# A routed trunk layer: second norm on VectorE and ScalarE, early expert splits on VectorE, and a re-ordered routing stage

## The chip, the cores and the metric

The kernel runs on one core of one Trainium2 chip. The metric is the device time of one execution in microseconds; the median of the runs counts. A trace names five engines: PE (TensorE matmuls; PEld is its weight load), DVE (VectorE), ACT (ScalarE), POOL (GpSimd) and SP (SyncE, which here only issues DMAs). Each engine works through a queue of its own, in order.

## What is computed

One layer on 1024 tokens of width 1024 in float32: a token mixer, a cross-attention into 256 memory tokens, and a mixture of 16 experts of which each token takes two. Each is followed by a residual norm. The part that matters here, cut from the reference:

```python
x = layer_norm(ALPHA * x + xa, ln_x_g, ln_x_b)         # second norm
scores = sigmoid(x @ router_w)                          # [T, 16]
sel = scores + router_bias
grp_score = top_k(sel.reshape(T, 4, 4), 2)[0].sum(-1)   # best of 4 groups
in_grp = group_of_expert == argmax(grp_score)
_, idx = top_k(where(in_grp, sel, -inf), 2)             # two experts in it
gate = take(scores, idx); gate = gate / gate.sum(-1)
y = sum over the two experts of gate * (silu(x@wg) * (x@wu)) @ wd
x = layer_norm(ALPHA * x + y, ln_moe_g, ln_moe_b)
```

Tokens are sorted by expert into blocks of 128 rows; a block is one gather, two matmul groups and one scatter with addition.

## The kernel before, in words

Tokens go in 8 tiles of 128. Every float32 product is three matmuls of a high and a low part (lines 78 to 80), so every operand is split: ACT copies the high part (line 74), another engine subtracts to get the low part (line 75).

The stage in question runs from the attention output to the first expert blocks. Its order is written out by hand: `at(time, fn, ...)` (line 600) files a step under a nominal time, and `run_agenda` (line 603) emits all steps sorted by it, so the nominal times fix the order within each engine's queue and nothing else. Steps of tile t:

- `p_turn`, `p_hi`, `p_lo` (from line 1212): transposed attention weights and their split. `xa` (line 1223): 48 matmuls into a PSUM tile; tile 7 is done in two halves (`xa_half`).
- Second norm. `n_sum` (line 1235) adds the residual on DVE, `n_stats` takes mean and variance on DVE (`bn_stats`), `n_scale` (line 1260) is one power on POOL. Then for tiles 0 to 5 `n_shift` (DVE), `n_norm` (ACT, line 1268), `n_affine` (POOL, line 1272) and `n_add` (POOL for tiles 0 to 3, DVE for 4 and 5; line 1275); for tiles 6 and 7 `n_vec`, two DVE passes (lines 1280 and 1281).
- `x_store`, `a_scale`, `a_store`: normed rows to DRAM, and scaled rows to the result buffer.
- Routing. `r_turn`, `r_copy`, `r_logits`, `r_score`: transpose, 16 small matmuls, sigmoid. `r_group` and `r_pick` (lines 874 and 889): 15 small DVE steps that choose two experts. `r_rank`: a small matmul with the counts so far. `r_place` (line 962, its steps from line 916): some 22 DVE steps that turn ranks into one-hot rows; `r_list` and `r_add` add them to the slot lists.
- After tile 3: `f_counts` to `f_gather` (from line 1034) choose three experts, fill two blocks from the first 512 tokens, and start weight loads (`f_load`, `fetch_some`: three register loads and five 1 MB DMAs on SP).
- `e_split` (line 1369) splits the 12 weight pieces of the first two experts: ACT for the high part, POOL for the low. `eb_*` are the two early blocks (products into `gup`, gate, transpose, fold, products into `yp`, scatter).
- After tile 7, placing is woven with `order_steps` (line 1160), then `o_sum`, `o_lists`, `o_index`, `o_gather` (from line 1176) give the slot lists and gather the next block. From there 20-odd blocks follow in a program order of the framework's own scheduler.

Of the kernel before, what the change touches and what calls it, by code (L numbers as in the profile page):

```python
# [9 lines left out]
F32 = mybir.dt.float32  # L10
F32R = mybir.dt.float32r
BF16 = mybir.dt.bfloat16
# [27 lines left out]
NEARLY = 3  # L40


@with_exitstack
def trunk_kernel(ctx: ExitStack, tc: tile.TileContext, a, out):
# [555 lines left out]
    def at(time, fn, *args):  # L600
        agenda.append((time, len(agenda), fn, args))
# [272 lines left out]
    def r_group(t):  # L874
        R = routes[t]
        sel, q, h = tt(f"rsel{t}", NE), tt(f"rq{t}", 12), tt(f"rh{t}", 8)
        R["sel"], R["g8"], R["gi"], R["gf"] = sel, tt(f"rg{t}", 8), tt(f"rgi{t}", 8, U32), tt(f"rgf{t}", 1)
        vec.tensor_tensor(sel, R["s"], rb, op=ALU.add)
        pr = sel[:, :].rearrange("p (g a b) -> p g a b", g=4, a=2)
        q3, h3 = q[:, :].rearrange("p (g a) -> p g a", a=3), h[:, :].rearrange("p (g a) -> p g a", a=2)  # L880
        vec.tensor_tensor(h3, pr[:, :, :, 0], pr[:, :, :, 1], op=ALU.max)
        vec.tensor_tensor(q3[:, :, :2], pr[:, :, :, 0], pr[:, :, :, 1], op=ALU.add)
        vec.tensor_tensor(q3[:, :, 2], h3[:, :, 0], h3[:, :, 1], op=ALU.add)
        vec.reduce_max(gs8[:, :4], q3, axis=AX.X)
        vec.max(R["g8"], gs8)
        vec.max_index(R["gi"], R["g8"], gs8)
        vec.tensor_copy(R["gf"], R["gi"][:, :1])

    def r_pick(t):
        R = routes[t]  # L890
        pen, ms_ = tt(f"rpen{t}", 4), tt(f"rms{t}", NE)
        vec.tensor_scalar(pen, iota16[:, :4], R["gf"], -BIG, op0=ALU.not_equal, op1=ALU.mult)
        vec.tensor_tensor(ms_[:, :].rearrange("p (g a) -> p g a", g=4), R["sel"][:, :].rearrange("p (g a) -> p g a", g=4),
                          pen[:, :, None].to_broadcast([P, 4, 4]), op=ALU.add)
        e8, ei, ef = tt(f"re{t}", 8), tt(f"rei{t}", 8, U32), tt(f"ref{t}", 2)
        vec.max(e8, ms_)
        vec.max_index(ei, e8, ms_)
        vec.tensor_copy(ef, ei[:, :2])
        oh, ohs = tt(f"roh{t}", NE), tt(f"rohs{t}", NE, BF16)
        vec.tensor_scalar(oh, iota16, ef[:, :1], None, op0=ALU.is_equal)  # L900
        vec.scalar_tensor_tensor(ohs, iota16, ef[:, 1:2], oh, op0=ALU.is_equal, op1=ALU.add)
        R["ef"], R["ohs"] = ef, ohs
# [13 lines left out]
    def place_steps(t):  # L916
# [27 lines left out]
        yield lambda: r_count(t)  # L944
# [86 lines left out]
    # the first experts are chosen, and two blocks filled, from the tokens seen by then  # L1031
# [40 lines left out]
    def f_close():  # L1072
# [3 lines left out]
        vec.tensor_copy(gce, m[:, NE + 2:NE + 4])  # L1076
        fill = first["fill"]
# [3 lines left out]
        first.update(idx=ixe, gate=gce)  # L1081
# [156 lines left out]
    def n_tiles(t):  # L1238
        S["ln", t] = [tiny.tile([P, n], F32, tag=g, name=f"{g}_n2_{t}") for g, n in (("mv", 2), ("sc", 1), ("nb", 1))]
        S["st", t] = tiny.tile([P, 2, 6], F32, tag="st", name=f"st_n2_{t}")  # L1240

    def n_moments(t):
        mv, sc, _ = S["ln", t]
        vec.bn_aggr(mv, S["st", t])
        vec.tensor_scalar(sc, mv[:, 1:2], EPS, None, op0=ALU.add)

    def n_stats(t):
        n_tiles(t)
        for k in range(2):
            vec.bn_stats(S["st", t][:, k, :], x2(t)[:, k * 512:k * 512 + 512])  # L1250
        n_moments(t)

    def n_half(k):
        if k == 0:
            n_tiles(7)
        cols = slice(k * 512, k * 512 + 512)
        vec.scalar_tensor_tensor(x2(7)[:, cols], x1(7)[:, cols], ALPHA, S["xa", 7][:, cols], op0=ALU.mult, op1=ALU.add)
        vec.bn_stats(S["st", 7][:, k, :], x2(7)[:, cols])

# [4 lines left out]
    def n_shift(t):  # L1264
        mv, sc, nb = S["ln", t]
        vec.scalar_tensor_tensor(nb, mv[:, :1], -1.0, sc, op0=ALU.mult, op1=ALU.mult)

    def n_norm(t):
        mv, sc, nb = S["ln", t]
        act.activation(x2(t), x2(t), AF.Identity, bias=nb, scale=sc)  # L1270

    def n_affine(t):
        pool.tensor_tensor(x2(t), x2(t), gb2[0], op=ALU.mult)

    def n_add(t):
        (pool if t < 4 else vec).tensor_tensor(x2(t), x2(t), gb2[1], op=ALU.add)

    def n_vec(t):
        mv, sc, nb = S["ln", t]
        vec.scalar_tensor_tensor(x2(t), x2(t), mv[:, :1], gb2[0], op0=ALU.subtract, op1=ALU.mult)  # L1280
        vec.scalar_tensor_tensor(x2(t), x2(t), sc, gb2[1], op0=ALU.mult, op1=ALU.add)
# [11 lines left out]
    B0 = 15.0  # L1293
    for t in range(NT):
        B = B0 * t
        end = B + B0
        if t:
            at(B - 8.1, p_turn, t)
            at(B - 7.1, p_hi, t)
            at(B - 7.0, p_lo, t)  # L1300
        for j, o in enumerate((0, 3.0, 4.3, 5.6, 7.8, 9.5, 10.8, 13.0)):
# [5 lines left out]
        if t < 7:  # L1307
            at(end + 0.1, n_sum, t)
            at(end + 0.2, n_stats, t)
        else:  # L1310
            at(end - 0.5, n_half, 0)
            at(end + 0.1, n_half, 1)
            at(end + 0.2, n_moments, t)
        at(end + 0.3, n_scale, t)
        if t < 6:
            at(end + 3.25, n_shift, t)
            at(end + 3.3, n_norm, t)
            at(end + 4.0, n_affine, t)
            at(end + 7.5, n_add, t)
            x, lg, group, pick, _, rank, place, late = (end + o for o in (10.6, 16.3, 18.1, 18.3, 21.3, 24.1, 24.6, 29.3))  # L1320
        elif t == 6:
            at(end + 0.4, n_vec, t)
            x, lg, group, pick, _, rank, place, late = (end + o for o in (6.0, 16.5, 20.8, 20.9, 20.95, 22.0, 22.2, 25.5))
        else:
            at(end + 0.4, n_vec, t)
            x, lg, group, pick, _, rank, place, late = (end + o for o in (5.3, 7.8, 10.8, 11.0, 12.95, 12.9, 13.3, 16.0))
        at(x + 0.1, x_store, t)
        turn_at = x + 0.3 if t == 7 else end + (12.1 if t < 6 else 15.2)
        at(turn_at, r_turn, t)
        at(turn_at + 1.0, r_copy, t)  # L1330
        at(turn_at + 2.0, a_scale, t)
        at(turn_at + 3.0, a_store, t)
        at(lg, r_logits, t)
        at(lg + 1.7, r_score, t)
        at(group, r_group, t)
        at(pick, r_pick, t)
        at(rank, r_rank, t)
        if t < 7:
            at(place, r_place, t)
        else:  # L1340
            at(place, lambda: r_place(7, order_steps()))
        at(late, r_list, t)
        if t < 7:
            at(late + (3.6 if t < 6 else 6.1), r_add, t)
        if t == 3:
            f = late + 3.7
            at(rank + 1.0, f_counts)
            at(rank + 4.0, f_choose)
            at(f + 0.1, f_slots)
            at(f + 0.2, f_bonus)  # L1350
# [3 lines left out]
            at(f + 0.5, f_load)  # L1354
            at(f + 0.6, fetch_some, 5)
# [21 lines left out]
    at(E - 14.5, early_splits)  # L1377
# [3 lines left out]
    for n, k in enumerate((6, 7, 8, 9)):  # L1381
        at(E + (-7.0, 0.35, 0.4, 0.45)[n], e_split, k, pool)
    for n, k in enumerate((4, 5, 10, 11)):
        at(E + 2.0 + 3.6 * n, e_split, k, pool)
# [37 lines left out]
    for n, base in ((0, E - 13.0), (1, E - 6.0)):  # L1422
        at(base, eb_turn, n)
        at(base + (1.0 if n else 1.4), eb_parts, n)
    for j in range(NK):
        at(E + (0.15, 0.2, 1.45, 1.46, 1.47, 5.0, 5.75, 5.76)[j], eb_hidden, 0, j)
# [200 lines left out]
```

## Time and profile before

| | us |
|---|---|
| median of 3 runs (994.6 to 996.63) | 996.24 |
| profiled execution, span from first to last instruction | 991.4 |
| its PE busy | 910.8 (92%) |
| its DVE busy | 584.9 (59%) |
| its ACT busy | 410.9 (41%) |
| its POOL busy | 304.2 (31%) |

The profiled execution has no time of its own beside its span; the median lies 4.8 us above the span, which is what lies around the first and the last instruction. Matmuls are pipelined and overlap in the records, so a busy PE says that work was queued. A row of a timeline is start, duration, engine, line, operation, output<-inputs, shapes and count, and in brackets the idle time before it with what ended it.

### The profile page before, as it was taken

Reading aid. Unit: us, or ns where it says so; the run is one execution under the profiler, and the core shown is the slowest. Engines: PE = TensorE matmul, PEld = TensorE weight load, DVE = VectorE, ACT = ScalarE, POOL = GpSimd, SP = SyncE. Lnnn points to the kernel's source line nnn. Section 1 sums busy time; section 2 is a strip of 40 time slices with the busy share of each in tenths; the row PEclk is TensorE's granted clock in tenths of the full one; section 3 lists DMA queues with packets and bytes.
Section 4 is the critical chain, followed back from the end, with each engine's and each line's share of the span. In section 5 each row is a group of like instructions: output and inputs, shape, how many; then the busy total and the mean of one; then the engine's idle time right before and its main releaser. Section 6 shows DMA issues by size and latency. Waiting matters only on the chain. (4 is left out here: it accounts for less than half of the span.)

```text
span 991.4 us, 13027 instructions
## 1 busy us (share of the span) xinstructions
PE 910.8 (92%) x4841; PEld 774.9 (78%) x4841; DVE 584.9 (59%) x1154; ACT 410.9 (41%) x640; POOL 304.2 (31%) x221
## 2 busy tenths in 40 slices
PE   8999999999899999999999999987589999999910
PEld 8999778788677889998888888876468888888710
DVE  5300374546876785272224558979957677676528
ACT  5311432245422144352224432234237667767524
POOL 0211243226453314201111042325732323333226
PEclk9999999999999999999999999999799999999965
DMA  8200011113421357420001012173549898898364
GB/s 304 83 22 22 22 65 43 64 32 128 170 75 54 107 194 273 150 86 0 1 1 43 1 43 86 64 310 108 190 128 347 298 317 290 281 296 270 51 196 167
DMA packets 35439, 133.41 MB, mean 135 GB/s; under 512 B 6640, under 2 KB 8240, under 8 KB 29232
## 3 DMA queue, kind: packets, MB, share of 16 engines
q1 hardware_dynamic: 28464, 115.79, 32.3%
q0 software_dynamic: 6912, 16.79, 7.2%
q8 instruction: 38, 0.62, 0.2%
q14 instruction: 25, 0.20, 0.1%
HBM read 115.75 MB, written 25.20 MB: 142 GB/s over the span
## 5 line engine op out<-in xcount | busy, mean ns | idle before, releaser
L75 DVE TENSOR_TENSOR ew<-raw,ew 128x1024 fp32r<-128x1024 f32 x84 | 101.5, 1223 | 21.7 <-ACT ew L74 20.8
L74 ACT ACTIVATE ew<-raw 128x1024 fp32r<-128x1024 f32 x96 | 100.3, 1057 | 19.4 <-PE xa L80 9.7
L78 PE MATMUL gup<-ew,xbT 128*128 128x512 f32 x192 | 79.2, 412 | 0.0
L1146 POOL DMA_INDIRECT yd<-y,idx x22 | 41.5, 1884 | 122.2 <-ACT ew L74 46.2
L79 PE MATMUL gup<-ew,xbT 128*128 128x512 f32 x192 | 76.7, 399 | 0.0
L80 PE MATMUL gup<-ew,xbT 128*128 128x512 f32 x192 | 76.7, 399 | 0.0
L78 PE MATMUL zB<-xs,wb 128*128 128x512 f32 x192 | 76.5, 399 | 0.0
L80 PE MATMUL zB<-xs,wb 128*128 128x512 f32 x192 | 76.1, 396 | 0.0
L79 PE MATMUL zB<-xs,wb 128*128 128x512 f32 x192 | 75.0, 391 | 0.0
L78 PE MATMUL xa<-vws,T_p 128*128 128x512 f32 x128 | 53.9, 421 | 0.0
L78 PE MATMUL mixp<-wm,mx 128*128 128x512 f32 x128 | 53.2, 415 | 0.0
L79 PE MATMUL mixp<-wm,mx 128*128 128x512 f32 x128 | 50.9, 398 | 0.7 <-DVE wm L75 0.7
L79 PE MATMUL xa<-vws,T_p 128*128 128x512 f32 x128 | 51.4, 401 | 0.0
L80 PE MATMUL xa<-vws,T_p 128*128 128x512 f32 x128 | 51.3, 401 | 0.0
L80 PE MATMUL mixp<-wm,mx 128*128 128x512 f32 x128 | 50.9, 398 | 0.0
L78 PE MATMUL sc<-As,T_x 128*128 128x512 f32 x128 | 50.9, 398 | 0.0
L80 PE MATMUL sc<-As,T_x 128*128 128x512 f32 x128 | 50.4, 394 | 0.0
L79 PE MATMUL sc<-As,T_x 128*128 128x512 f32 x128 | 50.2, 392 | 0.0
L791 POOL TENSOR_TENSOR pss<-pss,nm 128x1024 f32<-128x1024 f32 x8 | 15.1, 1894 | 113.2 <-DVE nm L789 113.2
L80 PEld LDWEIGHTS gup<-ew,xbT 128*128 128x128 f32 x192 | 36.8, 192 | 8.5
L78 PEld LDWEIGHTS gup<-ew,xbT 128*128 128x128 f32 x192 | 37.0, 193 | 7.9 <-issue 0.6
L79 PEld LDWEIGHTS zB<-xs,wb 128*128 128x128 f32 x192 | 36.1, 188 | 8.9 <-issue 0.5
(447 smaller groups left out, 2505.2 us busy)
## 6 DMA issues: line engine op xcount, KB each, us to landing
raw<-in_wgu SPq DMA_DIRECT2D x32, 1024.0 KB, 8.2
raw<-in_wdn SPq DMA_DIRECT2D x16, 1024.0 KB, 7.4
raw_wk<-in_wkv SPq DMA_DIRECT2D x16, 512.0 KB, 4.5
wbr<-in_wB SPq DMA_DIRECT2D x12, 512.0 KB, 3.2
xt<-in_x SPq DMA_DIRECT2D x8, 512.0 KB, 3.2
raw_wq<-in_wxqT SPq DMA_DIRECT2D x8, 512.0 KB, 4.2
xd<-x2s SPq DMA_DIRECT2D x8, 512.0 KB, 3.3
yd<-xal SPq DMA_DIRECT2D x8, 512.0 KB, 2.8
```

Source lines behind the costliest of these rows:

```text
L74: act.activation(hi, src, AF.Copy)
L75: sub.tensor_tensor(lo, src, hi.bitcast(F32), op=ALU.subtract)
L78: pe.matmul(ps, lhi, rhi, start=first, stop=False)
L79: pe.matmul(ps, lhi, rlo, start=False, stop=False)
L80: pe.matmul(ps, llo, rhi, start=False, stop=last)
L791: pool.tensor_tensor(pr4, pr4, nm[:, 1, :, None].to_broadcast([P, H, M]), op=ALU.mult)
L1146: pool.indirect_dma_start(out=yd[:, :], out_offset=bass.IndirectOffsetOnAxis(ap=ix, axis=0), in_=y[:, :D], in_offset=None, bounds_check=T ...
```

## The change

It touches this stage only. In words:

- Second norm of tiles 0 to 6: `n_sum` also gives the row sum, ACT squares the centred rows (`n_square`, written over the attention output in PSUM), DVE does `n_var`, `n_centre` and `n_vec`. POOL keeps the power alone. Tile 7 keeps `bn_stats`.
- The low parts of the 12 early weight pieces are subtracted on DVE (`vec`), at new places in the order.
- `r_group` and `r_pick` become one list of steps. For tile 7 it is woven with the placing steps of tile 6. `place_part` also runs for tile 6.
- `r_count` leaves the placing and follows `r_rank`.
- Times: tiles 15.4 apart instead of 15.0; transposes of the attention weights some 3 earlier; logits of a tile one tile earlier; early-expert choice and weight loads before the place of tile 3; the early blocks' steps and the two products of the second one later. `eb_store(0)` comes before `o_gather`, `eb_out(1)` after it.

Core of the diff:

```diff
+MOVES = {('e_split', k): -1.50 for all 12 k, ('place_last',): 2.50, ('xa', 5, 3): -1.00}
...
 def at(time, fn, *args):
+    time += MOVES.get((fn.__name__, *[a for a in args if isinstance(a, int)]), 0.0)
...
+    def r_choose(t):
+        beside = list(place_steps(t - 1)) if t == 7 else []
+        for n, step in enumerate(choose_steps(t)):
+            step()
+            for _ in range(2 if n % 2 and beside else 1):
+                if beside:
+                    beside.pop(0)()
+        for step in beside:
+            step()
...
     def n_sum(t):
-        vec.scalar_tensor_tensor(x2(t), x1(t), ALPHA, S["xa", t], op0=ALU.mult, op1=ALU.add)
+        vec.scalar_tensor_tensor(x2(t), x1(t), ALPHA, S["xa", t], ..., accum_out=sc)
+        vec.tensor_scalar(mv[:, :1], sc, -1.0 / D, None, op0=ALU.mult)
+    def n_square(t):
+        act.activation(S["xa", t], x2(t), AF.Square, bias=mv[:, :1], accum_out=mv[:, 1:2])
+    def n_var(t):
+        vec.tensor_scalar(sc, mv[:, 1:2], 1.0 / D, EPS, op0=ALU.mult, op1=ALU.add)
-    def n_norm(t):
-        act.activation(x2(t), x2(t), AF.Identity, bias=nb, scale=sc)
-    def n_affine(t):
-        pool.tensor_tensor(x2(t), x2(t), gb2[0], op=ALU.mult)
-    def n_add(t):
-        (pool if t < 4 else vec).tensor_tensor(x2(t), x2(t), gb2[1], op=ALU.add)
+    def n_centre(t):
+        vec.scalar_tensor_tensor(x2(t), x2(t), mv[:, :1], gb2[0], ...)
     def n_vec(t):
-        vec.scalar_tensor_tensor(x2(t), x2(t), mv[:, :1], gb2[0], op0=ALU.subtract, op1=ALU.mult)
         vec.scalar_tensor_tensor(x2(t), x2(t), sc, gb2[1], op0=ALU.mult, op1=ALU.add)
...
-    B0 = 15.0
+    B0 = 15.4
         if t < 7:
+            at(end + 22.6, place_part, t, 0)
+            at(end + 22.65, place_part, t, 1)
...
-    for n, k in enumerate((0, 1, 2, 3)):
-        at(E - 13.5 + 1.4 * n, e_split, k, pool)
...
+    for k, o in zip((0, 1, 2, 3, 6, 7, 8, 9, 4, 5, 10, 11), (-20.5, -18.5, -7.5, -7.4, -2.0, 2.2, 9.0, 13.5, 17.2, 17.3, 23.1, 23.2)):
+        at(E + o, e_split, k, vec)
```

In the new order the DVE queue from the end of tile 6's attention product reads: choice of tile 5, list of tile 4, norm of tile 6, count, low part of block 0, splits 2 and 3, placing of tile 5, first half of tile 7's sum, split 6, low part of block 1, choice of tile 6, list of tile 5, second half of tile 7's sum, `n_centre`, split 7, `n_vec`, count, gate product of block 0, placing of tile 6, split 8, fold of block 0, choice of tile 7 with a second placing of tile 6, split 9, count, splits 4 and 5, placing of tile 7 with the order steps, list of tile 6, gate product of block 1, `o_sum`, splits 10 and 11, `o_index`.

## Rows read from the trace of the kernel before

**Rows 1.** The page, busy tenths in 40 slices of the span and the granted clock

```profile
DVE  5300374546876785272224558979957677676528
POOL 0211243226453314201111042325732323333226
PEclk9999999999999999999999999999799999999965
```

**Rows 2.** Stretches: us, then busy PE, PEld, DVE, ACT, POOL; PEclk, DMA share, GB/s

```profile
662.40:687.60 25.20, 18.73 (x85) 15.20 (x84) 24.22 (x62) 9.92 (x12) 14.29 (x6) 0.86 0.58 197
687.60:732.60 45.00, 30.95 (x143) 24.84 (x144) 37.35 (x124) 13.81 (x18) 22.39 (x11) 0.85 0.33 117
732.60:945.00 212.40, 210.96 (x1045) 173.15 (x1046) 142.84 (x159) 143.95 (x173) 65.80 (x43) 0.99 0.83 264
```

**Rows 3.** Waits of PE from 640 to 735: total us, times, longest

```profile
PE rp L906 <- DVE rohs L901: 12.7, 2, 8.1
```

**Rows 4.** Timeline of DVE and of POOL around the second norm of tile 6

```profile
667.25 1.28 DVE L1280 SCALAR_TENSOR_TENSOR x2s<-x2s,mv_n,g 128x1024 f32<-128x1024 f32 x1
669.00 3.40 DVE L1281 SCALAR_TENSOR_TENSOR x2s<-x2s,sc_n,b 128x1024 f32<-128x1024 f32 x1 [0.46 <-POOL sc_n L1262]
...
667.42 1.54 POOL L1262 TENSOR_TENSOR sc_n<-sc_n,mhalf 128x1 f32<-128x1 f32 x1 [8.86 <-DVE sc_n L1245]
668.95 5.70 POOL L75 TENSOR_TENSOR ew<-raw,ew 128x1024 fp32r<-128x1024 f32 x2
```

**Rows 5.** DVE groups by shape, 662.4 to 723.5: busy us, mean ns | idle before

```profile
L1281 DVE SCALAR_TENSOR_TENSOR x2s<-x2s,sc_n,b 128x1024 f32<-128x1024 f32 x2 | 6.8, 3390 | 0.9 <-POOL sc_n L1262 0.9
L940 DVE TENSOR_SCALAR one<-iota,rpm,rgp 128x128 fp32r<-128x128 f32 x13 | 5.8, 502 | 0.0
L878 DVE TENSOR_TENSOR rsel<-rs,rb 128x16 f32<-128x16 f32 x3 | 3.9, 1313 | 0.0
L892 DVE TENSOR_SCALAR rpen<-iota,rgf 128x4 f32<-128x4 f32 x3 | 3.3, 1091 | 0.1
L957 DVE TENSOR_TENSOR rgp<-rgt,rgp 128x2 fp32r<-128x2 f32 x4 | 2.9, 721 | 0.0
L900 DVE TENSOR_SCALAR roh<-iota,ref 128x16 f32<-128x16 f32 x3 | 2.7, 913 | 0.1
L883 DVE TENSOR_TENSOR rq<-rh 128x4 f32<-128x4 f32 x3 | 2.6, 865 | 0.0
L881 DVE TENSOR_TENSOR rh<-rsel 128x8 f32<-128x8 f32 x3 | 2.6, 863 | 0.1
L898 DVE CAST ref<-rei 128x2 f32<-128x2 uint32 x3 | 2.3, 763 | 0.1
...
L937 DVE TENSOR_SCALAR one<-iota,rcd 128x128 fp32r<-128x128 f32 x8 | 2.2, 281 | 0.0
...
L882 DVE TENSOR_TENSOR rq<-rsel 128x8 f32<-128x8 f32 x3 | 0.5, 159 | 0.0
```

**Rows 6.** Timeline of DVE: a split's subtraction, a placing, the next sum

```profile
659.73 1.22 DVE L1221 TENSOR_TENSOR T_p<-tp_p,T_p 128x1024 fp32r<-128x1024 f32 x1
660.86 0.23 DVE L929 SCALAR_TENSOR_TENSOR rjunk<-iota,ref,rs 128x16 f32<-128x16 f32 x1
...
664.37 1.21 DVE L1236 SCALAR_TENSOR_TENSOR x2s<-x1s,xa 128x1024 f32<-128x1024 f32 x1
```

**Rows 7.** Timeline of ACT: first sigmoid's table load; a squaring in the last stage

```profile
585.04 1.28 ACT L872 ACT_TABLE_LOAD   x1
959.94 1.15 ACT L1550 ACTIVATE zscratch<-yl,zs 128x1024 f32<-128x1024 f32 x1 [0.47 <-DVE zs L1548]
```

**Rows 8.** Timeline of PE: two router products, and the next block's transposes

```profile
647.14 1.85 PE L867 MATMUL rp<-rw,x2T 128*128 128x16 f32 x16
710.81 3.43 PE L867 MATMUL rp<-rw,x2T 128*128 128x16 f32 x16
...
732.63 2.71 PE L390 MATMUL tp_xb<-ident,xbs 128*128 128x128 f32 x11 [2.10 <-DMA xbs<-xd,idx]
```

More of the change, by code (lines that the diff above doesn't have):

```diff
@@ L40 @@
 NEARLY = 3
+MOVES = {
+    ('e_split', 0): -1.50,
+    ('e_split', 1): -1.50,
+    ('e_split', 10): -1.50,
+    ('e_split', 11): -1.50,
+    ('e_split', 2): -1.50,
+    ('e_split', 3): -1.50,
+    ('e_split', 4): -1.50,
+    ('e_split', 5): -1.50,
+    ('e_split', 6): -1.50,
+    ('e_split', 7): -1.50,
+    ('e_split', 8): -1.50,
+    ('e_split', 9): -1.50,
+    ('place_last',): 2.50,
+    ('xa', 5, 3): -1.00,
+}
 @with_exitstack
@@ L889, in r_pick @@
-    def r_pick(t):
-        R = routes[t]
[L891 to L902, printed above, removed]
+        pen, ms_ = tt(f"rpen{t}", 4), tt(f"rms{t}", NE)
@@ L904, in r_rank, with place_part @@
+    def place_part(t, part):
+        R = routes[t]
+        if part == 0:
+            R["steps"] = list(place_steps(t))
+        for step in R["steps"][:9] if part == 0 else R["steps"][9:]:
+            step()
     def r_rank(t):
@@ L1076, in f_close, with f_fill @@
         vec.tensor_copy(gce, m[:, NE + 2:NE + 4])
+        first.update(idx=ixe, gate=gce)
+    def f_fill():
         fill = first["fill"]
@@ L1258, in n_half, with n_moments @@
         vec.bn_stats(S["st", 7][:, k, :], x2(7)[:, cols])
+    def n_moments(t):
+        mv, sc = S["ln", t]
+        vec.bn_aggr(mv, S["st", t])
+        vec.tensor_scalar(sc, mv[:, 1:2], EPS, None, op0=ALU.add)
     def n_scale(t):
@@ L1297, in trunk_kernel @@
         if t:
[L1298 to L1301, printed above, removed]
+            at(B - 11.2, p_turn, t)
+            at(B - 10.1, p_hi, t)
+            at(B - 9.0, p_lo, t)
+        for j, o in enumerate((0, 1.4, 2.8, 5.3, 6.7, 9.2, 12.5, 13.9)):
             if t < 7:
@@ L1307, in trunk_kernel @@
         if t < 7:
+            at(end + 22.6, place_part, t, 0)
+            at(end + 22.65, place_part, t, 1)
             at(end + 0.1, n_sum, t)
-            at(end + 0.2, n_stats, t)
+            at(end + 0.2, n_square, t)
+            at(end + 0.35, n_centre, t)
+            at(end + 0.3, n_var, t)
+            at(end + 0.32, n_scale, t)
+            at(end + 3.0, n_vec, t)
+            x, turn_at, lg, group, rank, late = (end + o for o in (6.6, 8.4, 10.9, 12.9, 18.4, 29.3))
         else:
-            at(end - 0.5, n_half, 0)
+            at(end - 5.0, n_half, 0)
@@ L1312, in trunk_kernel @@
             at(end + 0.1, n_half, 1)
             at(end + 0.2, n_moments, t)
[L1314 to L1326, printed above, removed]
+            at(end + 0.3, n_scale, t)
@@ L1327, in trunk_kernel @@
+            at(end + 0.35, n_centre, t)
+            at(end + 3.0, n_vec, t)
+            x, turn_at, lg, group, rank, late = (end + o for o in (5.2, 6.0, 8.0, 10.2, 13.4, 20.0))
         at(x + 0.1, x_store, t)
-        turn_at = x + 0.3 if t == 7 else end + (12.1 if t < 6 else 15.2)
         at(turn_at, r_turn, t)
         at(turn_at + 1.0, r_copy, t)
-        at(turn_at + 2.0, a_scale, t)
-        at(turn_at + 3.0, a_store, t)
+        at(turn_at + 2.2, a_scale, t)
+        at(turn_at + 3.3, a_store, t)
@@ L1333, in trunk_kernel @@
         at(lg, r_logits, t)
-        at(lg + 1.7, r_score, t)
-        at(group, r_group, t)
-        at(pick, r_pick, t)
+        at(lg + 0.5, r_score, t)
+        at(group, r_choose, t)
         at(rank, r_rank, t)
+        at(rank + (0.1 if t == 7 else 0.5), r_count, t)
+        if t == 7:
+            at(rank + 0.2, place_last)
+        at(late if t != 6 else end + 31.0, r_list, t)
         if t < 7:
-            at(place, r_place, t)
-        else:
-            at(place, lambda: r_place(7, order_steps()))
@@ L1342, in trunk_kernel @@
-        at(late, r_list, t)
-        if t < 7:
-            at(late + (3.6 if t < 6 else 6.1), r_add, t)
+            at(late + 1.0 if t != 6 else end + 31.5, r_add, t)
         if t == 3:
-            f = late + 3.7
-            at(rank + 1.0, f_counts)
-            at(rank + 4.0, f_choose)
+            f = late + 4.5
+            at(rank + 2.0, f_counts)
+            at(rank + 3.5, f_choose)
             at(f + 0.1, f_slots)
-            at(f + 0.2, f_bonus)
             at(f + 0.3, f_close)
@@ L1353, in trunk_kernel @@
             at(f - 8.0, gather_space)
-            at(f + 0.5, f_load)
-            at(f + 0.6, fetch_some, 5)
+            at(rank + 3.8, f_bonus)
+            at(rank + 3.9, f_fill)
+            at(rank + 3.6, f_load)
+            at(rank + 3.7, fetch_some, 5)
         if t == 7:
```

104 lines of the change are left out of this document (51 added, 53 removed).

## The prediction

> **What bounds the kernel now.** I read the page's slices first, then stretches, then PE's waits, then DVE and POOL side by side. In the slices [rows 1] DVE's digits rise to 9 in slices 27 to 29 (669 to 719 us), POOL's rise to 5 there, and the granted clock falls to 7: the end of the routing stage. Up to about 640 us and from 736 us PE is the bound. The stretches show it [rows 2]: from 732.6 to 945 PE is busy 210.96 of 212.40 us, but from the end of tile 6's attention product (662.4) to the transposes of the first block that needs the final lists (732.63, [rows 8]) it is busy 18.73 + 30.95 = 49.7 of 70.2 us. DVE is busy 24.22 of 25.20 in the first part and 37.35 of 45.00 in the second; its idle time lies almost all after 723. PE's longest wait is for `rohs`, the last step of an expert choice on DVE: 12.7 us in two waits [rows 3]. So the stage ends when DVE's queue ends, and everything after 732.63 shifts with it: the later blocks are PE-bound, and their weight loads start when pieces of the blocks before are split, so they shift too.
>
> **What is slow on DVE.** Nine groups of steps have means far above their size [rows 5]. Tile 6's last norm pass took 3.40 us; it began 0.05 us after a POOL subtraction began, while the pass before it, of the same size, took 1.28 [rows 4]. A 16-column step takes 0.23 or 0.16 undisturbed ([rows 6] L929, [rows 5] L882), yet `rsel` has a mean of 1.31; 128 columns take 0.28 (L937), yet the L940 group of the gates has 0.50. In this stretch POOL subtracts the low parts of 12 weight pieces. Mean less undisturbed, times count, with 1.28, 0.28, 0.17, 0.23, 0.16, 0.23, 0.17, 0.17 and 0.17 in the order of the rows: 4.2 + 2.9 + 3.4 + 2.6 + 2.2 + 2.0 + 2.1 + 2.1 + 1.8 = 23.3 us. Small steps overlap by some tenths in their records, so I take 22 as the part on the path.
>
> **The change, part by part** (sum over the 70.2 us of DVE's queue from 662.4 to 732.63):
>
> 1. The subtractions leave POOL, and the norm's two POOL passes go. POOL keeps powers, one memset and the gathers. The stretching goes: -22.0. Lower bound of the gain 18, since powers, gathers and scatters stay; upper 23.3.
> 2. The subtractions on DVE cost 1.13 each (659.73 to the next start 660.86, [rows 6]). Two run before the stretch, eight come ahead of the end of tile 7's placing: +9.0. The last two stand between `o_sum` and `o_index`; the list product that `o_index` waits for takes about 1.1 of their 2.3: +1.2. Their high parts on ACT are covered: ACT is busy 23.7 of 70.2 us [rows 2].
> 3. The diff places tile 6 twice: `place_part` runs for it, and the weave runs all its steps again. A placing takes 664.37 - 660.86 = 3.5 us [rows 6]. In the weave the choice's 15 steps, some 3.1 us alone because each waits about 0.2 for the one before, would fill with placing steps. I take 5.0 for both, so +1.9 on the path. Bounds +1.2 (perfect fill) and +3.5 (none).
> 4. Norm. For tile 6, sum, mean, squaring on ACT (1.15, [rows 7]) with two hand-overs, variance, centring (1.28), then the last pass after the power; POOL's power beside the centring took 1.54 and DVE idled 0.46 [rows 4]. That makes 6.2 against 5.8 with `bn_stats` undisturbed (664.37 to 669.00, [rows 4, 6], and 1.2): +0.4. While ACT squares, DVE waits and everything behind it in the queue too: about 1.4 per tile. For tile 7 split 7 stands in the power's wait: -0.5. For tiles 0 to 5 this chain ends about 7 us after the tile's product, and PE reaches the transpose some 7.7 us after it (30 large matmuls and 8 transposes ahead of it, at the 0.2 us of the later blocks, 212.4/1045 [rows 2]), so PE hides it; without that cover it costs PE the difference per tile. The squares are written over the attention output, whose PSUM tile stays taken about 1.4 us longer; its next user comes 7.7 us after, so nothing.
> 5. Head start. The old queue at 662.4 still held the rest of tile 4's placing (2.0, to 664.37 [rows 6]), tile 4's list (0.5) and tile 5's choice (3.1). In the new order those come before tile 6's sum; I work out that DVE is then 3.5 us behind PE: 5.6 - 3.5 = -2.1. Bounds -4 and 0.
> 6. PE ahead of that point. A router product moves one tile forward and so falls before 662.4: +1.7 (1.85 less its overlap, [rows 8]); one list product likewise 0.35; PE's small waits for the early choice I put 0.4 lower: +1.6. Bounds 0 and +3.
>
> Edits at nothing: the earlier transposes of attention weights (same PE work, a free PSUM tile); `r_count` alone (0.1 us either way). The early choice moves a tile forward with its three register loads and five 1 MB DMAs. They sit ahead of tile 4's `x_store` on SP, which waits some 3 us for the choice; nobody needs those rows until the late gathers. On DVE the 3 us of choice and bonus steps now come before tile 3's placing and make its list product wait about half a us (within part 6). Splits 1, 3 and 5 start the next loads on SP; by the order above split 5 ends 13 us ahead of block 2, whose own weights are split by then. `eb_store(0)` now goes ahead of the gathers on POOL, with about 4 us to spare; if it were late it would cost its 1.6 us. The second early block's output products move behind the gather, where PE was waiting anyway.
>
> Sum: -22.0 + 9.0 + 1.2 + 1.9 + 0.4 - 0.5 - 2.1 + 1.6 = **-10.5 us**. Against the profiled execution that is a span of 980.9; against the median, 4.8 above the span of before, 985.7.
>
> **A rule against the change.** The row of a table load reads 1.28 us [rows 7], and ACT has Sigmoid active when it squares tiles 1 to 6. The Trainium skill (ScalarE: Activation LUTs, "Table sets: the hidden batching unit") says functions come in sets, and the cheap ones it lists as present in every set do not include Square; its section on what a load costs gives about 2.66 us for a switch with its drain. No row squares beside Sigmoid. What the trace has is squaring in the last stage with the table of Silu active and no load before it [rows 7]. This is rival C.
>
> **Rivals.**
>
> A, the sum above: DVE's queue stays the bound and loses its stretching. For it: the rows of stretched steps beside POOL passes. Its own range: part 1's bounds give -1.3 to +4, part 3's -0.7 to +1.6, part 5's -1.9 to +2.1, part 6's -1.6 to +1.4; not all at once: 981 to 990.
>
> B, PE's clock. At 1.2 GHz the same router product took 3.43 instead of 1.85 [rows 8], and the grant was 0.85 over the end of the stage [rows 2]. In the new order 24 large matmuls stand between tile 7's rank and its list product. At half clock they cost 0.2 us more each (their mean in the later blocks again), 4.8, of which about 1 is covered: about 989.5. For: PE still idles some 4 us before tile 7's transpose. Against: the small products after it keep PE occupied again from there.
>
> C, table loads: two per tile around each squaring, 1.28 each. Tiles 4 to 6 lie where DVE lags, 3 x 1.3; the first four push the transpose past PE's 7.7 us by 0.6 each: +6.3, 992. By the page's 2.66, the same working gives about 1002.
>
> D, slower: DVE's long steps are not due to POOL's passes but belong to the small steps in this crowded order. Then part 1 falls away and the subtractions are added to the same queue: -10.5 + 22.0 = +11.5, 1007.7. It decides at the point where more than 10.5 of the 22 us (48%) stay. For: the long steps hit different lines in each tile. Against: the same line is short in one tile and long in another, and the long ones begin within a POOL pass.
>
> E, no change: the end of DVE's queue is shortened, but block 2 waits for something else, its gather or the loads of the third expert (issued after split 5). Price: what is gained is waited for, 996. Against: split 5 comes 13 us ahead, and the gather is issued by the end of DVE's queue itself.
>
> **How the numbers follow.** Chances: A 0.63, B 0.14, C 0.05, D 0.11, E 0.07. About 0.2% (2 us) is what a measurement of this kernel can tell from no change. A, B and C are faster by more: 0.82; E is the same: 0.07; D slower: 0.11. The time is A's, 985.7. The range 980 to 993 takes in A with its bounds, B and C, and leaves out E and D.
>
> **What would show it.** Right: no DVE step of 16 columns above 0.7 us between tile 5's norm and `o_index`; POOL busy under 10 us in the stage; PE reaching tile 6's end 1 to 2 us later than 662.4 and block 2's transposes near 722; the weave some 5 us long; no second table load in ACT's timeline before Silu. Wrong: long steps that remain with POOL idle (D); the products of the early blocks at 0.43 us each up to the last list product (B); `n_square` behind a table load (C); a PE wait for a gather or a weight load ahead of block 2 (E); a PE wait at the transposes of tiles 0 to 3, which would say that the norm's chain has no cover.

## The result, and the profile after

The changed kernel took 979.84 us (median of 4, 978.75 to 981.74) against 995.42 us before on the same chip: 0.985 of the time, 95% interval 0.9832 to 0.9867, 15.6 us faster by the medians. The forecast was 985.7 with 980 to 993, a gain of 10.5. The direction and the path were right; the median lies 0.2 us below the lower end of the range, with a gain some 5 us larger than forecast. In part that is luck: later runs of the same kernel showed that 979 to 982 is only one of its two groups of times, and all four runs here fell into it, where only 3 of the next 12 did (experiment 5).

The page of the profiled execution: span, busy times, and three of the lines of 40 slices.

```profile
span 976.9 us, 13063 instructions
...
PE 906.3 (93%) x4841; PEld 769.5 (79%) x4841; DVE 569.9 (58%) x1190; ACT 411.7 (42%) x648; POOL 252.2 (26%) x199
...
DVE  6300375445877777362224637788967667776528
...
POOL 0211243225544323300111001020032322332226
PEclk9999999999999999999999999998899999999965
```

Against [rows 1], POOL's digits in the stage fall to 0 to 2, and DVE reaches 9 in one slice where it did in three. POOL is busy 52 us less, DVE 15 us less although it took over twelve subtractions.

Two stretches are used below for every kernel. The **stage** runs from PE's first attention product (xa) to the transposes of block 2 (tp_xb); the **block loop** from there to the last gate/up product (gup). Two rows of the changed kernel by tile, the first matmul line of xa and of gup (count; shortest, median and longest in ns; first and last start):

```profile
L97 PE MATMUL xa<-vws,T_p x128: 388/394/796, 559.2 to 683.8; 128*128 128x512 f32 x128
L97 PE MATMUL gup<-ew,xbT x192: 387/394/774, 685.1 to 922.3; 128*128 128x512 f32 x192
```

and PE's timeline at the transposes of blocks 2, 3 and 4, with the wait ahead of each in brackets:

```profile
719.57 1.06 PE L409 MATMUL tp_xb<-ident,xbs 128*128 128x128 f32 x8 [1.88 <-DMA xbs<-xd,idx]
721.28 1.06 PE L409 MATMUL tp_xb<-ident,xbs 128*128 128x128 f32 x8 [0.64 <-DMA xbs<-xd,idx]
727.74 1.03 PE L409 MATMUL tp_xb<-ident,xbs 128*128 128x128 f32 x8
```

The stage took 719.6 - 559.2 = 160.4 us. Before, the first xa started at 559.4 and the transposes at 732.63 [rows 8]: 173.2. So the stage gave 12.8 us. The loop took 202.7 against 203.6, and the last stage, which combines and norms, gave another half a us.

On the path, from the end of tile 6's product to `o_index` (the windows view, from 103.0 us after the first xa, which is that end before and 1.1 us ahead of it here: length, busy time of PE, PEld, DVE, ACT and POOL, granted clock, DMA share, GB/s), the changed kernel reads

```profile
662.20:713.86 51.66, 44.12 (x204) 34.33 (x203) 47.76 (x207) 20.78 (x26) 4.64 (x3) 0.87 0.48 161
```

and the kernel before

```profile
662.40:727.60 65.20, 46.76 (x217) 37.98 (x217) 60.73 (x181) 22.62 (x28) 33.18 (x14) 0.84 0.43 150
```

DVE is still the bound: busy 47.8 of 51.7 us, where it was 60.7 of 65.2. It issues more instructions there (207 records against 181) and is busy 13 us less. POOL's 33.2 us are gone.

### The profile page after: what moved, and what is told of

Its sections match the earlier page's. It is cut to its first block, busy times and chain, and to the rows that moved or that the text cites. A ratio compares the mean times of both kernels' runs of the same rounds, so it can differ in the third digit from the quotient of the medians.

```text
span 976.9 us, 13063 instructions
## 1 busy us (share of the span) xinstructions
PE 906.3 (93%) x4841; PEld 769.5 (79%) x4841; DVE 569.9 (58%) x1190; ACT 411.7 (42%) x648; POOL 252.2 (26%) x199
## 5 line engine op out<-in xcount | busy, mean ns | idle before, releaser
L94 DVE TENSOR_TENSOR ew<-raw,ew 128x1024 fp32r<-128x1024 f32 x96 | 115.8, 1222 | 21.6 <-ACT ew L93 20.5
L1182 POOL DMA_INDIRECT yd<-y,idx x22 | 37.4, 1701 | 99.8 <-DMA yd<-y,idx 34.5
L1300 POOL TENSOR_TENSOR sc_n<-sc_n,mhalf 128x1 f32<-128x1 f32 x8 | 11.8, 1476 | 128.9 <-DVE sc_n L1283 111.6
L99 PEld LDWEIGHTS gup<-ew,xbT 128*128 128x128 f32 x192 | 36.8, 192 | 8.8 <-DVE xbT L1141 0.2
```

The source lines that it names most:

```text
L94: sub.tensor_tensor(lo, src, hi.bitcast(F32), op=ALU.subtract)
L99: pe.matmul(ps, llo, rhi, start=False, stop=last)
L1182: pool.indirect_dma_start(out=yd[:, :], out_offset=bass.IndirectOffsetOnAxis(ap=ix, axis=0), in_=y[:, :D], in_offset=None, bounds_check=T ...
L1300: pool.tensor_tensor(sc, sc, mhalf[:, :1], op=ALU.pow)
```

## The experiments

Five questions: is POOL's work what stretched DVE (1, 2), what do norm and order bring (3), what does the doubled placing cost (4), why does the changed kernel have two groups of times (5), and what is a better version (6). All ratios are to the kernel before on the same chip. The table gives each profiled execution's stage and loop, read as above, beside its time; where the runs of a kernel fall apart, the profile's own time is what goes with stage and loop. The changed kernel has three profiles, and their stages run from 159.3 to 160.4: a difference of less than about 1 us between two single profiles says little, so comparisons with that kernel give both ends.

| kernel | stage | loop | profiled run | median | ratio (95%) |
|---|---|---|---|---|---|
| before | 173.2 | 203.6 | | 995.4 | 1 |
| before, new norm | 170.3 | 207.2 | 993.6 | 997.2 | 1.0005 (0.9991 to 1.002) |
| before, low parts on DVE | 166.5 | 207.7 | 991.9 | 992.8 | 0.9965 (0.9952 to 0.9977) |
| before, both | 163.3 | 206.1 | 989.8 | 986.4 | 0.9885 (0.9865 to 0.9904) |
| changed | 160.4 | 202.7 | 978.8 | 979.8 | 0.985 (0.9832 to 0.9867) |
| changed, second time | 159.3 | 210.9 | 986.6 | 986.4 | 0.9869 (0.9835 to 0.9903) |
| changed, third time | 159.4 | 209.1 | 986.3 | 986.7 | 0.9907 (0.9885 to 0.9929) |
| changed, seven low parts on POOL | 168.3 | 206.4 | 992.3 | 990.4 | 0.9929 (0.9909 to 0.995) |
| changed, tile 6 placed once | 158.6 | 209.6 | 985.8 | 984.8 | 0.986 (0.9831 to 0.9888) |
| changed, no weave | 157.9 | 202.9 | 977.5 | 979.3 | 0.982 (0.9798 to 0.9842) |
| changed, loads late | 160.1 | 203.0 | 979.3 | 985.3 | 0.9879 (0.9847 to 0.9912) |
| changed, store later | 159.4 | 202.8 | 980.7 | 981.0 | 0.9863 (0.9848 to 0.9877) |
| changed, no weave, store later | 157.7 | 204.2 | 979.0 | 979.6 | 0.9844 (0.9831 to 0.9857) |

### 1. Seven subtractions back on POOL

```diff
-        at(E + o, e_split, k, vec)
+        at(E + o, e_split, k, pool if k in (0, 1, 2, 3, 6, 7, 8) else vec)
```

> The changed kernel with the low parts of seven early weight pieces (0, 1, 2, 3, 6, 7, 8) subtracted on POOL again; five of them fall into the stretch after tile 6's attention product. Theory A (POOL's subtractions stretch DVE's steps): DVE saves 5 x 1.13 = 5.7 us, but each subtraction on POOL stretches what DVE does beside it, by 22/10 = 2.2 us a piece in the sum, 11 us: about 5 us slower than the changed kernel (985), between +2 and +8, with 16-column steps of 1 us and more on DVE while POOL subtracts. Theory D (the long steps belong to the crowded order, not to POOL): DVE's queue only loses 5.7 us and the kernel is some 5 us faster than the changed one (974). Theory E (block 2 waits for something else): no difference, 980.

Measured: 990.44, ratio 0.9929. Against the changed kernel's first ratio (0.985) that is 7.9 us slower, against its second and third (0.9869 and 0.9907, which hold the slower group of experiment 5) 6.0 and 2.2. The stage, which that group hardly touches, is plainer: 168.3 us against 159.3 to 160.4, some 8 to 9 us longer. That is theory A's sign, at or above the upper edge of its size; by D it would have been faster. Its timeline around three of POOL's passes, DVE's rows and then POOL's:

```profile
677.77 0.16 DVE L985 SCALAR_TENSOR_TENSOR rcd<-rkk,ref 128x2 f32<-128x2 f32 x1
677.85 2.37 DVE L986 SCALAR_TENSOR_TENSOR rpm<-rkk,rrank 128x2 f32<-128x2 f32 x1
680.14 2.41 DVE L987 TENSOR_SCALAR rgt<-rgt 128x2 f32<-128x2 f32 x1
682.47 0.28 DVE L972 TENSOR_SCALAR one<-iota,rcd 128x128 fp32r<-128x128 f32 x1
...
682.93 2.33 DVE L991 TENSOR_TENSOR rgp<-rgt,rgp 128x2 fp32r<-128x2 f32 x1
...
677.78 4.74 POOL L94 TENSOR_TENSOR ew<-raw,ew 128x1024 fp32r<-128x1024 f32 x2 [3.54 <-ACT ew L93]
682.88 2.36 POOL L94 TENSOR_TENSOR ew<-raw,ew 128x1024 fp32r<-128x1024 f32 x1 [0.36 <-ACT ew L93]
```

This is no slowing by a share. A step of two columns lasts as long as POOL's whole pass: it begins at 677.85, POOL's pass at 677.78, and both end near 680.2 (half of the two passes' 4.74 us); the next step is held for the second pass, one more for the third. From 677.85 to 685.26 DVE got six short steps done in 7.4 us. A long step waits for the pass and then runs its own time: the norm's last pass began 0.06 us after a subtraction of 2.38 and took 3.41, as in [rows 4].

Not every step is held. Before, from 600 to 728 us, the longest `MAX8` took 0.18, `FIND_INDEX8` 0.17 and `TENSOR_REDUCE` 0.17, while `TENSOR_TENSOR` came to 2.42, `TENSOR_SCALAR` to 2.27 and `CAST` to 1.95. The Trainium skill (SBUF — State Buffer, "Who interferes with whom") says this: DVE and GpSimd share a pair of ports under an exclusive lock, a DVE step with at most one input in SBUF stays out of it, and copies, casts and `tensor_scalar` can still take it through their two-port modes. By that rule the trace agrees in the rows named here.

### 2. The low parts alone, in the kernel before

```diff
-        at(E - 13.5 + 1.4 * n, e_split, k, pool)
+        at(E - 13.5 + 1.4 * n, e_split, k, vec)
```

and likewise for the other two groups of pieces.

> The kernel before with one edit: all twelve low parts on DVE, in the places where POOL's subtractions were issued. Theory A: the stretch (22 us) goes, ten to eleven subtractions of 1.13 us come (11 to 12): about 10 us faster than before (985), and no 16-column step above 0.7 us after tile 6's product. Theory D: DVE's queue gets 11 to 12 us longer and nothing is saved: 1007. Theory E: 995.

Measured: 992.84, ratio 0.9965: 3.5 us faster, between A and E. The window from tile 6's product to `o_index`:

```profile
663.30:720.85 57.55, 45.27 (x217) 37.31 (x216) 51.80 (x193) 22.49 (x28) 2.94 (x2) 0.85 0.48 170
```

DVE is busy 51.80 us instead of 60.73, with all twelve subtractions in the window (12 x 1.13 = 13.6). So 8.9 + 13.6 = 22.5 us of stretching went; the prediction's first term was 22.0. The mechanism and its size hold. But of the 8.9 us the time shows 3.5. DVE's idle time in the window grew from 4.5 to 5.75, the step from `o_index` to the transposes of block 2 from 5.0 to 5.9, and that leaves the stage's 6.7. Then the loop lost some 4 us: PE stood 2.5 us at block 5's transposes for its gather,

```profile
746.26 0.66 PE L390 MATMUL tp_xb<-ident,xbs 128*128 128x128 f32 x4 [2.48 <-DMA xbs<-xd,idx]
```

a gather that POOL had issued at 733.66, behind two 1 MB weight loads of 730.77 and a scatter of 731.76: 12.6 us. The other 1.6 us lie right behind the wait, where PE's granted clock was 0.58 (746.3 to 750.0) and its matmuls took 0.63 us in place of 0.39. What is won ahead of the loop can be lost to a transfer in it.

### 3. The norm alone, and both

The first has the new norm for tiles 0 to 6 in the old order; the second adds the edit of experiment 2.

```diff
-            at(end + 0.2, n_stats, t)
+            at(end + 0.2, n_square, t)
+            at(end + 0.25, n_var, t)
...
+        at(end + 0.35, n_centre, t)
+        at(end + (3.0 if t < 6 else 0.4), n_vec, t)
...
-            at(end + 3.25, n_shift, t)
-            at(end + 3.3, n_norm, t)
-            at(end + 4.0, n_affine, t)
-            at(end + 7.5, n_add, t)
```

> The kernel before with the new norm for tiles 0 to 6 alone (sum with its accumulator, squaring on ACT, centring and scaling on DVE, only the power on POOL), the low parts still on POOL and the order as it was. By the sum the norm is worth +0.4 for tile 6 and nothing for the others, so within 2 us of before (993.5 to 997.5). Rival one: the old passes on POOL stretched DVE in tiles 0 to 5 too, so DVE reaches tile 6's end with a shorter queue: up to 4 us faster. Rival two: without the new order the norm's chain has no cover on PE in tiles 0 to 5, or DVE's waits for ACT's squares (1.4 us a tile) push everything behind them: 3 to 6 us slower.

> The kernel before with both: the new norm for tiles 0 to 6 and all low parts on DVE, in the old order, without the woven choice. If the parts add, it stands at the low-part run plus or minus the norm run's difference, about 985, and what is left to the changed kernel (980) is what the order is worth: 3 to 6 us. Rival: the order itself carries the gain; then this one is no faster than 991. Second rival: the order is worth nothing and the two edits alone reach 980.

Measured: the norm alone is no change (997.18, 1.0005); both are 0.9885 (986.42), 11.4 us faster by the ratio and 10.0 by the medians. So the norm is worth nothing by itself and 6 to 8 us in time beside the other edit. In the stage the parts do add: norm 2.9, low parts 6.7, both 9.9, and the order brings 2.9 to 4.0 more. The rest is the loop, 206 to 208 us in these three profiles against 203. For the norm alone the profiled run is the quickest of its runs, for both edits the slowest (table), so, by an estimate from these times that no profile shows, the usual loop of the one is longer by some 3.5 us and that of the other shorter: with both, the loop would be all but free of the loss, and the norm's gain appears. With the norm alone POOL issued block 5's gather at 738.60, and PE waited for it until 749.86. In the run with both, DVE is busy as long as in the changed kernel, and idle longer:

```profile
664.80:719.50 54.70, 44.00 (x214) 36.46 (x213) 48.00 (x182) 23.14 (x30) 2.99 (x2) 0.84 0.51 175
```

48.0 against 47.8 us busy, 6.7 against 3.9 idle. So in this window the order brings steps where DVE waited. Its busy time is the same only on balance: behind tile 6's product the changed kernel has ten of the twelve subtractions on DVE, where this one has all twelve, and one placing more.

### 4. The doubled placing and the weave

Tile 6 placed once, in the weave alone:

```diff
-            at(end + 22.6, place_part, t, 0)
-            at(end + 22.65, place_part, t, 1)
+            if t < 6:
+                at(end + 22.6, place_part, t, 0)
+                at(end + 22.65, place_part, t, 1)
```

> The changed kernel with tile 6 placed once, in the weave alone. By the sum the doubled placing lies on DVE's path in full: 3.4 us less there (692.3 to 695.7 in the changed kernel's trace), so o_index and block 2 come 3.4 us earlier: 976.4. Rival one: tile 7's choice can't begin before its scores (695.4) and the 0.4 us split of the hidden values, whose high part lands at 694.4, and the weight piece's high part at 694.1; then only about 1.5 us are won, 978.3. Rival two: PE, the scatter on POOL and the output products of the second early block set block 2's start by then, and less than 0.5 us is won.

Tile 6 placed once, ahead of tile 7's choice, and that choice alone (there is no tile 8, so nothing is woven in):

```diff
-        beside = list(place_steps(t - 1)) if t == 7 else []
+        beside = list(place_steps(t - 1)) if t == 8 else []
```

> The changed kernel with tile 7's choice alone, tile 6 placed once ahead of it (the weave taken out). The choice alone takes 3.05 us (tile 6's in the changed kernel), the weave 4.94: 1.9 us less on DVE's path, 978. Rival one: the choice alone waits more between its steps beside nothing, or PE's work ahead of the rank becomes the bound: no gain, 980. Rival two (the weave's point was to place tile 6 at no cost): slower, which would need the choice alone to be longer than 4.94.

The two medians can't be set against each other directly (984.78 and 979.33), since the first kernel's runs fall into the groups of experiment 5; one of its runs took 977.44. The stages can, as far as single profiles go: 158.6 and 157.9 against 159.3 to 160.4. `o_index` came 152.9 us after the first attention product in the one and 152.2 in the other, against 153.7 to 154.7. The placing that costs 3.43 by its rows was worth 0.6 to 1.7, between rival two and rival one: tile 7's choice has to wait for its scores in any case. Taking out the weave was worth 1.4 to 2.5: it costs more than it hides. It runs from 697.16 to 702.1 in the changed kernel, the choice alone from 697.22 to 700.3:

```profile
697.22 0.16 DVE L904 TENSOR_TENSOR rsel<-rs,rb 128x16 f32<-128x16 f32 x1
700.13 0.23 DVE L919 SCALAR_TENSOR_TENSOR rohs<-iota,ref,roh 128x16 bf16<-128x16 f32 x1
```

The change pays 4.9 us in place of 3.1 for a result that is already there.

### 5. Loads late; and two groups of times

```diff
-            at(rank + 3.6, f_load)
-            at(rank + 3.7, fetch_some, 5)
+            at(f + 0.5, f_load)
+            at(f + 0.6, fetch_some, 5)
```

(with `early_splits` at E - 25.0).

> The changed kernel with the loads of the early experts' weights issued where the kernel before issued them, after the first lists (f + 0.5 in the hand order, 12 us later), all else as it is. The prediction put the earlier loads at nothing. If they are worth nothing, 980 and PE busy in the block loop as before. Rival, read from the runs of the kernel before with single edits: blocks that start earlier with loads that did not start earlier meet more weight traffic, their gathers land after 9 to 12 us where the changed kernel has 6, and PE waits 2 to 4 us in the loop: 982 to 984. Second rival: the early blocks' own pieces come late and hold up DVE's queue in the routing stage: 985 or more, with DVE idle before the early splits.

> The changed kernel once more, as the measure for the three kernels that are compared with it on the same chip: 0.985 of before.

The late loads changed nothing that can be told: the profile has a stage of 160.1 and a loop of 203.0. But the six runs of that kernel lie between 979.3 and 988.4, and the changed kernel itself, run a second time beside it, took 978.7 and 980.9 in two runs and 986.2 to 988.5 in four (below: the lower and the upper group). The profiled run was one of the four (986.6). Its stage is even shorter (159.3), and its loop is 8.2 us longer. PE's transposes of blocks 2, 3 and 4 in it:

```profile
718.59 1.06 PE L409 MATMUL tp_xb<-ident,xbs 128*128 128x128 f32 x8 [0.30 <-DMA xbs<-xd,idx]
720.85 1.07 PE L409 MATMUL tp_xb<-ident,xbs 128*128 128x128 f32 x8 [1.19 <-DMA xbs<-xd,idx]
732.82 1.94 PE L409 MATMUL tp_xb<-ident,xbs 128*128 128x128 f32 x8 [5.37 <-DMA xbs<-xd,idx]
```

Block 4 stood 5.4 us waiting for its gather, where the run above had no wait at 727.74. POOL's queue (the second early block's scatter, the gathers of blocks 4 and 5) and the next weight loads on SP in that run:

```profile
719.72 1.61 POOL L1182 DMA_INDIRECT yd<-y,ixe  x1 [3.02 <-ACT y L1181]
721.64 1.04 POOL L1028 DMA_INDIRECT xbs<-xd,idx  x1 [0.31 <-issue]
722.98 0.99 POOL L1028 DMA_INDIRECT xbs<-xd,idx  x1 [0.30 <-issue]
...
722.11 1.24 SPq L854 DMA_DIRECT2D raw<-in_wgu  x2
```

and in the first profile of the changed kernel:

```profile
719.13 1.61 POOL L1182 DMA_INDIRECT yd<-y,ixe  x1 [1.55 <-ACT y L1181]
721.04 1.04 POOL L1028 DMA_INDIRECT xbs<-xd,idx  x1 [0.31 <-issue]
722.62 0.99 POOL L1028 DMA_INDIRECT xbs<-xd,idx  x1 [0.53 <-PE tp_xb L409]
...
724.21 1.25 SPq L854 DMA_DIRECT2D raw<-in_wgu  x2
```

The gather waits its turn behind the scatter in both. Where the two 1 MB loads start 0.5 us after it, it landed 11.0 us after its issue; where they start 3.2 us after it, in 5.8. The run with tile 6 placed once fits (loads at 722.95, gather at 723.08, landed in 10.2, PE's wait 5.3), and so does the one with late loads (3.2 us between them, landed in 5.7, no wait). Of the 8.2 us by which the loop is longer, 5.4 are this wait. Most of the rest follows it: from 732.8 to 737.8 PE's granted clock was 0.50, where the first profile has 1.00 at the same block, and the next block's transposes come 2.2 us later still.

Why the loads start earlier in the upper group can be followed two steps back. SP issues them behind 13 reads of the expert order into registers, which wait for the lists. The reads and two windows in the first profile:

```profile
L1234 SPq TENSOR_LOAD <-erow x13: 261/265/1390, 714.6 to 723.5; - x13
702.30:705.70 3.40, 3.40 (x10) 2.69 (x11) 3.40 (x5) 0.00 (x0) 0.00 (x0) 0.53 0.00 0
715.00:718.50 3.50, 2.58 (x10) 1.80 (x10) 0.07 (x1) 0.77 (x1) 2.04 (x2) 1.00 0.73 172
```

and in the second:

```profile
L1234 SPq TENSOR_LOAD <-erow x13: 262/266/1146, 713.7 to 721.4; - x13
702.30:705.70 3.40, 3.11 (x14) 2.34 (x14) 3.40 (x9) 0.26 (x1) 0.00 (x0) 1.00 0.00 0
715.00:718.50 3.50, 3.29 (x8) 1.98 (x7) 0.00 (x0) 0.17 (x1) 1.40 (x2) 0.52 0.64 168
```

In the upper run the reads begin 1.0 us earlier after the first attention product (154.4 against 155.4 us) and take 7.7 us in place of 8.9: together the 2.2 us. They begin earlier because the lists are ready earlier, and of that 1.0 us some 0.6 arise where PE's granted clock differs. In the first profile it was 0.53 ahead of the counts product that DVE's order steps wait for, after PE had idled 2.6 us; in the second it was 1.00 there, after an idle time of 0.8, and 0.52 in the last products of the second early block, whose scatter then came half a us later. The profile with late loads agrees with the first (0.56, reads of 8.9 us), the third one of the changed kernel with the second (1.00, 7.7 us). Why the clock falls at different places in one program, and why the 13 reads differ by 1.2 us, stays open.

So I moved the scatter, for a third pair of runs:

```diff
-    at(E + 28.4, eb_store, 1)
...
         split_some(3, ahead)
+        if n == 2:
+            eb_store(1)
```

> The changed kernel a third time, the measure for the two beside it. Its runs so far fall into two groups, 979 to 982 and 986 to 988; the trace of one of the upper group shows PE waiting 5.4 us for block 4's gather, which came behind the scatter of the second early block and 0.5 us ahead of two 1 MB weight loads. Both groups are expected again.

> The changed kernel with the second early block's result stored after the first weight pieces of block 2 are split, so that POOL issues block 4's gather ahead of that scatter, some 2 us or more ahead of the weight loads. Theory (the upper group is the gather caught behind scatter and loads): no run above 983, all at 979 to 981, and no PE wait above 2 us after block 2's transposes. Rival one: the upper group comes from something else, and it stays at 986 to 988 in half of the runs. Rival two: the scatter is now late and holds up later gathers or the loads: 983 and more in all runs.

Measured: the changed kernel again in both groups (980.74, 984.6, and four runs from 986.3 to 988.0), the edited one 980.69 to 981.52 in all four. POOL and SP in its trace:

```profile
718.09 0.99 POOL L1028 DMA_INDIRECT xbs<-xd,idx  x1 [0.30 <-issue]
722.36 0.99 POOL L1028 DMA_INDIRECT xbs<-xd,idx  x1 [3.28 <-PE tp_xb L409]
723.66 0.99 POOL L1028 DMA_INDIRECT xbs<-xd,idx  x1 [0.31 <-PE tp_xb L409]
...
731.82 1.62 POOL L1182 DMA_INDIRECT yd<-y,ixe  x1 [0.30 <-issue]
...
724.47 1.26 SPq L854 DMA_DIRECT2D raw<-in_wgu  x2
```

Block 4's gather goes 2.1 us ahead of the loads, the scatter 9.5 us later, and PE has no wait above half a us in blocks 2 to 4. This profile has the upper group's other marks: the loads start 162.9 us after the first attention product, as in the upper profiles of the changed kernel (162.8 and 162.9; 165.0 in the lower one), and the granted clock was 1.00 ahead of the counts product and 0.51 in the last early products. Only the places of the gather and the scatter on POOL differ, and the 6 to 8 us are gone. That the upper group is the caught gather is shown by this. How much of its delay comes from the scatter ahead of it and how much from the loads was not tried apart.

### 6. Both edits together

> The same, and tile 7's choice without the weave (tile 6 placed once, ahead of it). If both theories hold it is the fastest: the weave's 1.9 us off DVE's path, 977 to 979 in all runs, ratio to before about 0.981. Rival: the shorter list stage runs into the gather and the loads, and nothing is won over the store moved alone (979 to 981).

Measured: 979.64 (977.28 to 980.27), ratio 0.9844, beside 986.7 (0.9907) for the changed kernel on that chip. It is the fastest on that chip, though only two of its five runs lie in the 977 to 979 that were expected of all. The weave's share is small here, 1.4 us between the medians of this and the store alone, about the 1.7 us between their stages (157.7 and 159.4). Without the weave alone, POOL's order already had block 4's gather ahead of the scatter (719.03 and 720.32), and all five runs took 977.5 to 980.5; so the two fastest kernels are one finding, not two.

## Why the prediction was right, and where it was off

**The path** was right: DVE's queue from tile 6's product to `o_index`, cut by the stretching. **Part 1**, -22.0, measured 22.5 (experiment 2, in the old order). **Part 2**: eight subtractions came as counted, at 1.13 each; for splits 10 and 11 `o_index` followed `o_sum` by 2.74 us (711.12 to 713.86) against 1.71 in the run with both edits in the old order, +1.0 for +1.2. **Part 3**: the weave took 4.94 for the 5.0 taken; its price of 1.9 stands beside 1.4 to 2.4 us in `o_index`'s time without it. **Rival D** falls with experiments 1 and 2.

**Parts 4 and 5**, norm and head start, had -2.2 together, with the head start put down to the new order. The runs give the norm alone 2.9 us of the stage in the old order, so much of the head start can come from the norm. A row of before fits: DVE's last norm pass of tile 5, and all behind it in the queue, stood 3.5 us for the multiplication on POOL.

```profile
658.59 1.23 DVE L1276 TENSOR_TENSOR x2s<-x2s,b 128x1024 f32<-128x1024 f32 x1 [3.54 <-POOL x2s L1273]
```

With the norm alone that wait is gone, and DVE waits 0.8 us for PE at tile 6's sum. How much of the head start in the new order is the norm's was not tried apart. The chain of tile 6 itself is as worked out. DVE waits 1.39 for ACT's squares and 0.46 for the power:

```profile
665.71 1.22 DVE L1274 SCALAR_TENSOR_TENSOR x2s<-x1s,xa 128x1024 f32<-128x1024 f32 x1
...
668.51 0.15 DVE L1283 TENSOR_SCALAR sc_n<-mv_n 128x1 f32<-128x1 f32 x1 [1.39 <-ACT xa L1279]
668.58 1.27 DVE L1304 SCALAR_TENSOR_TENSOR x2s<-x2s,mv_n,g 128x1024 f32<-128x1024 f32 x1
...
670.32 1.28 DVE L1307 SCALAR_TENSOR_TENSOR x2s<-x2s,sc_n,b 128x1024 f32<-128x1024 f32 x1 [0.46 <-POOL sc_n L1300]
```

The sum began at 665.71, 2.4 us behind PE (663.3), where 3.5 had been worked out. **Part 6**: PE reached that point 0.9 us later than before, for +1.6.

**The 4.0 us by which the span's gain (14.5) passes the sum (10.5).** From PE's end of tile 6 to `o_index` the changed kernel takes 713.86 - 663.3 = 50.6 us for 65.2, -14.6, where parts 1 to 5 make -12.1: 1.1 of the 2.5 is the head start, 0.5 the stretching (as measured in experiment 2), 0.6 less idle time on DVE, and 0.3 is not accounted for. Part 6 gives 0.7 more; between `o_index` and the transposes 0.7 is lost. That is the stage. After it the transposes of blocks 2 and 3 stand closer together (0.9), and the end gives 0.5. This is the first profile, of the lower group. The forecast time also took 4.8 us for what lies around the first and the last instruction; in every run since, the time is only 1.7 to 2.2 us above the span (978.75 against 976.9). The rest of the 4.8 says that the profiled execution of before was a quick one, so the medians show a larger gain (15.6) than the spans (14.5).

**What the sum did not have** are DVE's waits for PE, which come forth once POOL's passes are gone: 6.7 us of idle time with both edits in the old order. The new order takes them back (3.9). The sum held DVE's idle time as it was (4.5), so two terms that it lacked nearly cancel, which is luck. The order, for which it had the head start and split 7 (-2.6) against the weave (+1.9), is worth 2.9 to 4.0 us in the stage with the weave in it.

**The step that failed** is the sentence that everything after block 2's transposes "shifts with it". It holds in the first profile (loop 202.7 against 203.6 before) and not in others: 206 to 208 with single edits, 209 to 211 in the upper group of the changed kernel. Rival E had the right resource, the gather, at the wrong block; its reason against ("the gather is issued by the end of DVE's queue itself") is true of block 2 and says nothing of block 4, whose gather stands behind a scatter on POOL and beside the loads. The prediction gave `eb_store(0)` 4 us to spare; it was `eb_store(1)` that mattered. Of the changed kernel's 16 runs, 7 lie at 978.7 to 981.7, one at 984.6 and 8 at 986.2 to 988.5.

**B** came true in small. Nothing hung on the granted clock of 0.79 from 680 to 700 us, since PE waited 2.6 us for tile 7's rank after it. But from 702.3 to 705.7 it was 0.53 in the first profile, the products behind that rank stood 0.43 us apart from 702.9 to 705.5, as B's sign had it, and DVE waited 0.5 us for the counts product behind them. In the second and third profile the clock was 1.00 there, and DVE came through that place 0.6 us earlier. So it cost about 0.6 us of the 3.8 that B put in. **C** fell: between the load ahead of the first Sigmoid and that of Silu, ACT's timeline has no other, and six squares lie between them, the last at 667.24:

```profile
582.09 1.28 ACT L892 ACT_TABLE_LOAD   x1
...
667.24 1.12 ACT L1279 ACTIVATE xa<-x2s,mv_n 128x1024 f32<-128x1024 f32 x1 [6.76 <-DVE mv_n L1275]
...
698.27 1.28 ACT L1422 ACT_TABLE_LOAD   x1
```

The Trainium skill (ScalarE: Activation LUTs, "Table sets: the hidden batching unit") does not name Square among the functions that every set has; here it ran between Sigmoids without a load. PE's waits at the transposes of tiles 0 to 3, the sign that the norm has no cover, did not appear. Of the signs of being right, no step of 16 columns took more than 0.4 us from 653 to 714 (0.7 had been allowed), POOL was busy 7.2 us from tile 6's product to the transposes (under 10), and the weave took 4.9. PE reached tile 6's end 0.9 us later (1 to 2), and block 2's transposes came at 719.57, 2.4 us ahead of the 722 named.

## What to carry to other kernels

Look for long steps that begin within a pass of POOL: a two-column step that takes 2.4 us is not slow, it is held, and moving POOL's pass to DVE at 1.13 us is cheaper than leaving it there. Then follow a gain past the stage where it is made, into the queues of transfers: here a gather behind a scatter and beside 1 MB loads cost 6 to 8 us, half of the gain, in half of the runs. Steps done twice and woven in "for nothing" have a price, and a trace shows it as the difference between two starts.

## What was not expected

- DVE is held by POOL for whole passes, and by kind of step: 2.3 to 2.4 us for steps of two columns, 5.42 us for one step of 128 columns that began at 659.19, beside a gather's issue on POOL, and lasted through the two passes behind it (experiment 1's kernel), and never for `MAX8`, `FIND_INDEX8` or the reduction.
- A gather's time to land goes with when loads start beside it: 10.2 to 11.0 us with two 1 MB loads within 0.6 us of it, 5.7 and 5.8 with 3.2 us between them (all behind a scatter).
- Runs of one program differ in where PE's granted clock falls. In the profiles of the changed kernel and of the one with late loads that goes with when lists and loads come, and so with whether the gather is caught; that the clock sets the group was not tried.
- PE waited 2.35 us ahead of tile 7's second half for the first half's sum on DVE (679.17), a wait that the order brings and that costs nothing, since DVE was behind PE there anyway; that it costs nothing was argued from DVE's queue, not tried.
